# Layer 1's second operand group in other homes and another order, one raw weight load later, and one token pair's transposes one product later

## The chip, the cores and the metric

The kernel runs on one core of a Trainium2 chip. The core has five engines that run their own instruction streams side by side: TensorE (PE, matmuls and transposes, with a separate line for its weight loads, PEld), VectorE (DVE), ScalarE (ACT), GpSimd (POOL) and SyncE (SP, which here issues the DMAs). They wait for one another by semaphores. The metric is the time of one execution on the device in microseconds (us), lower is better.

## The reference, cut to what is computed

One layer of an encoder: two groups of heads side by side (a bidirectional mLSTM and a latent attention), a projection of their outputs, and a feed-forward part. Sequence 2048, model width 1024, hidden width 4096, all in float32.

```python
h = rms_norm(x, g_mix_norm[l])
z = h @ w_in[l]
q_m, k_m, v_m, o_m, gates, c_q, c_kv, k_pe = jnp.split(z, splits, axis=-1)
...
y_a = mlstm_group(q_m, k_m, v_m, o_m, gates, b_gates[l], g_mlstm_out[l])
y_b = mla_group(c_q, c_kv, k_pe, cos, sin, g_cq[l], g_ckv[l], w_uq[l], w_ukv[l],
                g_q[l], g_k[l])
x = x + jnp.concatenate([y_a, y_b], axis=-1) @ w_out[l]
h = rms_norm(x, g_ffn_norm[l])
x = x + jnp.square(jax.nn.relu(h @ w_ff1[l])) @ w_ff2[l]
```

The change lies in the last three lines: in the projection by `w_out`, and in the product by `w_ff1`, which the kernel calls layer 1. Layer 2 is the product by `w_ff2`.

## The kernel before

**Arithmetic.** A float32 operand is split into a high part, rounded to the matmul's type, and a low part, the rest. ACT writes the high part (a copy, L53 or L1455, L1819, L1881), DVE the low part (a subtraction, L54 or L47). A product is the sum of three matmuls, high by high, high by low and low by high (`mm3`, L68 to L71). The three large products (projection, layer 1, layer 2) are block products in the manner of Strassen and Winograd: seven products of half-size blocks in place of eight, where some operands are sums and differences of blocks, named S1 to S4 and T1 to T4, beside the plain blocks A11, B21 and so on.

**Order.** From the projection on, the program order is written by hand: each engine executes its instructions in the order in which the Python code issues them, and waits only where data or memory requires it. Python code that stands later on the page can thus hold an engine up only if it is later on the same engine.

**Projection (class OutProj, `run`).** Sixteen token tiles of 128 rows go in eight pairs, `PAIRS`; the first is done plainly, and the loop over n = 1 to 7 does seven products for each other pair. Between the products the loop issues the work of the neighbours: for pair n the operands (`cast`, `low`, `combine`), for pair n - 1 (named p, with the token tiles a1 and b1) the sum with x (`add`, L1407), the store, the norm (`squares`, POOL's root, `scale`, L1495) and the transposition of the normalised rows: `transpose_n` (L1505, four PE transposes of half a token tile into the one PSUM buffer `dpt`) and `evacuate_n` (L1509, DVE, out of that buffer and times the gain). Pair p's normalised blocks then go through `combine_store` to DRAM (`d_h`), as the seven operands of layer 1. With n = 2, p is the first pair that takes this way, and product 6 of pair 1 stands between products 1 and 2 of pair 2. In the last round, n = 7 (`LAST`), the loop also reads back and splits layer 1's operands (`h_load` L1853, `h_split`) and loads the first two raw weight blocks (`load_w1`, L1795, two loads of 512 KB for a unit).

**Layer 1 (class FeedForward, `layer1`).** The tokens are done in two groups of 1024, and the hidden width in 16 units of 256, so there are 32 units n, each of seven products p; the first group has units 0 to 15, the second 16 to 31. Product p reads operand p of the token group (`self.H[p]`) and the weights of the unit (`weights1`, a generator that splits them some products ahead and forms S1 to S4 by `w1_combine`, L1809). `evacuate` takes each product out of PSUM (DVE L1943, ACT L1946 and L1947), `u_combine` (L1980) forms layer 2's operands and `u_store` (L1974) sends them to DRAM (`d_u`).

The seven operands of a group lie in seven **homes**, pairs of high and low tiles named after `HSLOT`: B11, B21, T2, T1, T3, B22, B12, in this order for operands 0 to 6 of the first group. T1, T2 and T3 are in one pool (`f_h0`), the B homes in another (`f_h1`) on the other side of memory. The second group is brought in by the generator `exchange`, which runs over units 14 to 16: operand 0 goes to stage buffers, operand 1 to the ring, and operands 2 to 6 into the homes that the first group's products 0 to 4 of unit 15 leave one by one (B11, B21, T2, T1, T3). Each is loaded into the home's low tile (L1885, two loads), and `place`, called once per product, casts one half to the high tile (L1881) and subtracts it from the half before (L47). The list `todo` sets the order of these splits.

**Layer 2 (`layer2`).** It has 112 units of 24 matmuls (8 blocks of three). Its first two units are prepared early: `first2` loads them in unit 31, and `opening()`, called after product 4 of unit 31, closes the pool of T1, T2, T3 and opens the pools of layer 2 (`open2`) in the memory so freed, with the splits of the first two units into `uh`, `ul`, `w2h`, `w2l`. In program order, these splits stand ahead of the evacuations of products 4, 5 and 6 of unit 31. `start2` then closes the pool of the B homes and issues the loads of the third unit (L2091, L2097, L2144), and `layer2` issues those of unit n + 3 in unit n.

Of the kernel before, what the change touches and what calls it, by code (L numbers as in the profile page):

```python
# [1288 lines left out]
class OutProj:  # L1289
# [229 lines left out]
    def run(self, ff):  # L1519

        nc = self.c.nc
        LAST = len(self.PAIRS) - 1
        self.sw, self.xp = ff.sw, ff.r1p
        pieces = [(op, k) for op in range(7) for k in range(4)]

        def h_load(n):
            for _ in range(n):
                i = 28 - len(pieces)
                ff.h_load(0, *pieces.pop(0), self.c.e[:, i - 4, :] if 4 <= i < 8 else None)

        def h_split(n):
            for _ in range(n):
                ff.h_split()

        self.prep_y(1)
        for s in (2, 3):
            self.load_y(s)
        self.load_b2(1)
        for s in range(2):
            self.load_x(s)  # L1540
        self.load_b2(0)
        for s in (2, 3):
            self.load_x(s)
        tops = self.t_operands(ff.hp)

        def t_op(n):
            for _ in range(n):
                next(tops, None)

        self.project(0, [(j, k) for k in range(KD) for j in range(2)])  # L1550
        t_op(4)
        for s in (2, 3):
            self.transpose_y(s)
        self.project(1, [(j, k) for j in (1, 0) for k in range(KD)])
        t_op(2)
        self.cast(1, "A11")
        self.combine(1, "S1")
        self.low()
        self.combine(1, "S3")
        t_op(1)  # L1560
        self.cast(1, "A12")
        self.cast(1, "S1")
        self.low()
        self.low()
        t_op(1)
        for j in range(2):
            self.add(0, j, ("plain", 0, j), True)
        self.store(0)

        comb = iter(())  # L1570
        for n in range(1, LAST + 1):
            m, p = n + 1, n - 1
            a, b = 2 * n, 2 * n + 1
            a1, b1 = a - 2, b - 2
            a2, b2 = a + 2, b + 2
            norm, norm1, more = 1 <= n <= 4, 1 <= p <= 4, n < LAST

            self.product(n, 0)
            if n > 1:
                self.add(b1, 1, (p, "A"))  # L1580
            else:
                for j in (1, 0):
                    self.add(1, j, ("plain", 1, j), True)
                self.store(1)
            if norm1:
                self.scale(a1)
            self.combine(n, "S2")
            if n == 1:
                t_op(1)
            next(comb, None)  # L1590

            if n == LAST - 1:
                ff.load_w1(0)
            if n == 2:
                self.product(n, 1)
            elif n > 2:
                self.product(p, 6)
            if norm1:
                self.transpose_n(0)
            self.add(a, 0, (n, "A"))  # L1600
            if n == 2:
                t_op(2)
                self.product(p, 6)
            self.cast(n, "S2")
            self.cast(n, "A22")
            self.low()
            self.combine(n, "S4")
            self.low()
            self.cast(n, "S4")
            next(comb, None)  # L1610
            if more:
                self.load_y(a2)
                self.load_y(b2)
            else:
                ff.load_w1(1)
                h_load(2)

            if n != 2:
                self.product(n, 1)
            if norm1:  # L1620
                self.evacuate_n(a1, 0)
                self.transpose_n(1)
            if n > 1:
                self.add(b1, 0, (p, "A"), True)
                self.store(b1)
            if norm1:
                self.squares(b1)
            self.low()
            for _ in range(2):
                next(comb, None)  # L1630
            if n == 1:
                t_op(1)
            if n == LAST:
                h_split(2)

            self.product(n, 2)
            self.add(a, 0, (n, "B"), True)
            self.cast(n, "S3")
            if norm1:
                self.scale(b1)  # L1640
                self.evacuate_n(a1, 1)
                self.transpose_n(0)
            if n == 1:
                t_op(2)
            if n == LAST:
                h_split(3)
            if n >= LAST - 1:
                h_load(2 if more else 4)

            self.product(n, 3)  # L1650
            self.add(*((b, 1, (n, "C")) if more else (a, 1, (n, "A"))))
            self.low()
            if norm1:
                self.evacuate_n(b1, 0)
                self.transpose_n(1)
            if more:
                self.transpose_y(a2)
                self.transpose_y(b2)
                self.load_x(a2)
            if n == 1:  # L1660
                t_op(1)
            if n == LAST:
                h_split(3)
            if n >= LAST - 1:
                h_load(2)

            self.product(n, 4)
            self.add(*((a, 1, (n, "A")) if more else (b, 1, (n, "C"))))
            if more:
                self.cast(m, "A11")  # L1670
                self.combine(m, "S1")
                self.low()
                self.combine(m, "S3")
                self.load_x(b2)
            if norm1:
                self.evacuate_n(b1, 1)
            if n == 1:
                t_op(1)
            if n == LAST:
                ff.wsteps = ff.weights1()  # L1680
                next(ff.wsteps)
                h_split(3)
            if n >= LAST - 1:
                h_load(2 if more else 3)

            self.product(n, 5)
            if more:
                self.add(a, 1, (n, "C"), True)
                self.store(a)
            else:  # L1690
                self.add(b, 1, (n, "A"))
            if more:
                self.cast(m, "A12")
                self.cast(m, "S1")
                self.low()
                self.low()
            if norm:
                self.squares(a)
            if norm1:
                comb = self.combine_store(p)  # L1700
            next(comb, None)
            if n == 1:
                t_op(1)
            if n == LAST:
                for _ in range(3):
                    next(ff.wsteps)
                h_split(3)
            if n >= LAST - 1:
                h_load(2 if more else 3)

        self.product(LAST, 6)
        self.add(a, 1, (LAST, "C"))
        self.store(a)
        for _ in range(2):
            next(ff.wsteps)
        h_split(2)
        h_load(2)
        next(ff.wsteps)
        self.add(b, 0, (LAST, "A"))
        self.store(b)  # L1720
        next(ff.wsteps)
        return pieces
# [41 lines left out]
class FeedForward:  # L1764
# [58 lines left out]
    def weights1(self):  # L1823

        N = 2 * self.NU
# [4 lines left out]
        for s in range(7 * N + 1):  # L1830
            if last:
                last()
                self.nsplit += 1
            last = self.w1_split(*divmod(s, 7)) if s < 7 * N else None
            yield
            n, q = divmod(s - 1, 7)
            if s and q == 0:
                self.w1_combine(n, "S3")
            elif s and q == 2:
                self.w1_combine(n, "S4")  # L1840
            elif q == 4 and n + 1 < N:
                self.w1_combine(n + 1, "S1")
            elif q == 5 and n + 1 < N:
                self.w1_combine(n + 1, "S2")
            elif s and q == 6 and n + 2 < N:
                self.load_w1(n + 2)
            yield

# [19 lines left out]
    def exchange(self):  # L1868
# [3 lines left out]
        todo = []  # L1872
# [24 lines left out]
        for _ in range(4):  # L1897
            place()
            yield
        nxt = [first, [[t[:, k, :] for t in s for k in range(2)] for s in second]]  # L1900
        for p in range(13):
            if p < 5:
                hi, lo = self.h_slot(p)
                nxt.append([[t[:, k, :] for k in range(4)] for t in (hi, lo)])
                for k in range(0, 4, 2):
                    load(hi[:, k:k + 2, :], lo[:, k:k + 2, :], c.d_h[1, p + 2, :, k:k + 2, :])
            if p < 7:
                self.H[p] = nxt[p]
            place()
            yield  # L1910
# [364 lines left out]
```

## Time and profile before

| | us |
|---|---|
| median of 3 runs | 2565.96 |
| lowest to highest | 2564.87 to 2566.89 |
| profiled execution, whole time | 2567.94 |
| its span | 2566.1 |
| mean granted clock of TensorE in it | 0.998 |

The profile comes from one execution. Its page gives the busy time of each engine and, for groups of instructions of one line, the mean duration and the idle time of the engine just before them with what ended it. The stages in time, by PE's rows of its timeline: the projection runs from about 1155 to 1327, layer 1 from 1327.32 to 1944.83, layer 2 from there to the end. Row by row, the timeline shows start, duration, engine, line, operation, the names of what is written and read, and in brackets the idle time ahead and its releaser.

### The profile page before, as it was taken

Reading aid. Unit: us, or ns where it says so; the run is one execution under the profiler, and the core shown is the slowest. Engines: PE = TensorE matmul, PEld = TensorE weight load, DVE = VectorE, ACT = ScalarE, POOL = GpSimd, SP = SyncE. Lnnn points to the kernel's source line nnn. Section 1 sums busy time; section 2 is a strip of 40 time slices with the busy share of each in tenths; the row PEclk is TensorE's granted clock in tenths of the full one; section 3 lists DMA queues with packets and bytes.
Section 4 is the critical chain, followed back from the end, with each engine's and each line's share of the span. In section 5 each row is a group of like instructions: output and inputs, shape, how many; then the busy total and the mean of one; then the engine's idle time right before and its main releaser. Section 6 shows DMA issues by size and latency. Waiting matters only on the chain. (4 is left out here: it accounts for less than half of the span.)

```text
span 2566.1 us, 37087 instructions
## 1 busy us (share of the span) xinstructions
PE 2541.2 (99%) x13148; PEld 2155.2 (84%) x13148; DVE 1726.2 (67%) x3300; ACT 1248.3 (49%) x2517; POOL 385.4 (15%) x430
## 2 busy tenths in 40 slices
PE   9999999999999999999999999999999999999999
PEld 7888888888888888898888888888887888888887
DVE  4585467766676667678788777977774577666443
ACT  5554444546656656565445555655553323332332
POOL 1111111123224214110100000000000233222000
PEclk9999999999999999999999999999999999999999
DMA  5434234356446454535786655744447644444552
GB/s 172 144 111 151 91 117 135 95 135 128 102 87 134 94 111 105 89 103 191 218 283 208 200 198 177 251 162 151 144 152 270 214 148 142 148 143 146 213 180 95
DMA packets 301790, 393.67 MB, mean 153 GB/s; under 512 B 33125, under 2 KB 186788, under 8 KB 301604
## 3 DMA queue, kind: packets, MB, share of 16 engines
q1 hardware_dynamic: 299140, 386.84, 50.1%
q10 hardware_dynamic: 2464, 4.46, 0.5%
q8 instruction: 103, 1.69, 0.3%
q14 instruction: 83, 0.68, 0.1%
HBM read 259.04 MB, written 132.17 MB: 152 GB/s over the span
## 5 line engine op out<-in xcount | busy, mean ns | idle before, releaser
L69 PE MATMUL pd<-w2h,uh 128*128 128x512 f32 x896 | 349.4, 390 | 3.5 <-DVE e L1943 3.5
L70 PE MATMUL pd<-w2l,uh 128*128 128x512 f32 x896 | 349.2, 390 | 1.8 <-DVE w2l L54 1.8
L71 PE MATMUL pd<-w2h,ul 128*128 128x512 f32 x896 | 349.0, 390 | 0.0
L54 DVE TENSOR_TENSOR ul<-ur,uh 128x1024 fp32r<-128x1024 f32 x110 | 146.9, 1335 | 254.7 <-ACT uh L53 254.6
L53 ACT CAST uh<-ur 128x1024 fp32r<-128x1024 f32 x110 | 116.0, 1055 | 397.2 <-PE pd L70 385.0
L54 DVE TENSOR_TENSOR ptl<-ptp,pth 128x512 fp32r<-128x512 f32 x252 | 173.6, 689 | 174.5 <-ACT pth L53 165.6
L53 ACT CAST pth<-ptp 128x512 fp32r<-128x512 f32 x252 | 146.4, 583 | 240.5 <-PE ptp L1120 235.2
L1943 DVE TENSOR_TENSOR e<-pu,e 128x512 f32<-128x512 f32 x224 | 150.9, 687 | 89.1 <-PE pu L71 88.1
L1080 DVE TENSOR_SCALAR_CACHE_REDUCE p<-ps 128x512 f32<-128x512 f32 x256 | 174.8, 683 | 47.1 <-PE ps L1079 39.0
L69 PEld LDWEIGHTS pd<-w2h,uh 128*128 128x128 f32 x896 | 168.6, 188 | 38.9 <-DVE e L1943 3.9
L70 PEld LDWEIGHTS pd<-w2l,uh 128*128 128x128 f32 x896 | 168.6, 188 | 37.2 <-DVE w2l L54 2.2
L71 PEld LDWEIGHTS pd<-w2h,ul 128*128 128x128 f32 x896 | 168.5, 188 | 35.1
L2107 POOL TENSOR_TENSOR r<-wr,r 128x512 f32<-128x512 f32 x48 | 86.3, 1797 | 622.0 <-DVE w2l L54 452.3
L69 PE MATMUL pz<-wh,hh 128*128 128x512 f32 (+1 forms) x384 | 150.1, 392 | 2.1 <-ACT hh L53 0.7
L1120 PE MATMUL ptp<-ident,p 128*128 128x128 f32 x1008 | 151.3, 273 | 0.7 <-ACT p L1091 0.7
L71 PE MATMUL pz<-wh,hl 128*128 128x512 f32 (+1 forms) x384 | 150.4, 392 | 0.0
L70 PE MATMUL pz<-wl,hh 128*128 128x512 f32 (+1 forms) x384 | 149.9, 391 | 0.1
L70 PE MATMUL pv<-ptl,vh 128*128 128x256 f32 x496 | 140.4, 283 | 1.4 <-DVE ptl L54 1.3
L1946 ACT ACTIVATE e<-e 128x512 f32<-128x512 f32 x128 | 80.9, 632 | 122.8 <-DVE e L1943 116.2
L71 PE MATMUL pv<-pth,vl 128*128 128x256 f32 x496 | 140.0, 282 | 0.0
L69 PE MATMUL pv<-pth,vh 128*128 128x256 f32 x496 | 139.9, 282 | 0.0
L1091 ACT ACTIVATE p<-p,nm 128x2048 f32<-128x2048 f32 x64 | 128.5, 2008 | 19.7 <-DVE nm L1084 19.7
(526 smaller groups left out, 6591.6 us busy)
## 6 DMA issues: line engine op xcount, KB each, us to landing
d_u<-e SPq DMA_DIRECT2D x224, 256.0 KB
ur<-d_u SPq DMA_DIRECT2D x110, 512.0 KB
wr<-in_w SPq DMA_DIRECT2D x96, 256.0 KB
w1raw<-in_w SPq DMA_DIRECT2D x42, 512.0 KB
raw<-in_w_in SPq DMA_DIRECT2D x48, 256.0 KB
r<-in_w SPq DMA_DIRECT2D x22, 512.0 KB
mb<-d_M SPq DMA_DIRECT2D x32, 256.0 KB
acc<-d_x SPq DMA_DIRECT2D x16, 512.0 KB
```

What stands on the lines that cost most here:

```text
L53: r = nc.scalar.copy(hi, src)
L54: (eng or nc.vector).tensor_tensor(lo, src, hi.bitcast(F32), op=ALU.subtract)
L69: nc.tensor.matmul(out, ah, bh, start=first, stop=False, skip_group_check=more)
L70: nc.tensor.matmul(out, ah, bl, start=False, stop=False, skip_group_check=more)
L71: nc.tensor.matmul(out, al, bh, start=False, stop=last, skip_group_check=more)
L1080: nc.vector.tensor_scalar(probs[b, a][:, j, :], o, SCALE, None, op0=ALU.mult, op1=ALU.max, accum_out=maxes[b, a][:, j:j + 1])
L1091: nc.scalar.activation(p, p, AF.Exp, bias=maxes.pop((b, a)), accum_out=dens[b][:, a:a + 1])
L1120: nc.tensor.transpose(pt[:, k, :], p[:, j, k * P:(k + 1) * P], c.ident)
L1943: nc.vector.tensor_tensor(out, o, t, op=ALU.add)
L1946: nc.scalar.activation(t, t, AF.Relu)
L2107: nc.gpsimd.tensor_tensor(R, wr, R, op=ALU.subtract)
```

## The change

It has three parts. None adds or removes an instruction; all move instructions within program order, and the second group's operands get other homes.

In the projection, only with n = 2: the four transposes of each half token tile, their evacuations and `scale(b1)` are issued one product later than before. The first transposes come after product 6 of pair 1, the last after product 4 of pair 2, and the last evacuation after product 5.

```diff
-            if norm1:
+            if norm1 and n > 2:
                 self.transpose_n(0)
             self.add(a, 0, (n, "A"))
             if n == 2:
                 t_op(2)
                 self.product(p, 6)
+                self.transpose_n(0)
...
-            if norm1:
+            if norm1 and n > 2:
                 self.evacuate_n(a1, 0)
                 self.transpose_n(1)
...
             self.cast(n, "S3")
-            if norm1:
+            if n == 2:
+                self.evacuate_n(a1, 0)
+                self.transpose_n(1)
+                self.scale(b1)
+            elif norm1:
                 self.scale(b1)
                 self.evacuate_n(a1, 1)
                 self.transpose_n(0)
...
-            if norm1:
+            if n == 2:
+                self.evacuate_n(a1, 1)
+                self.transpose_n(0)
+            elif norm1:
                 self.evacuate_n(b1, 0)
                 self.transpose_n(1)
...
-            if norm1:
+            if n == 2:
+                self.evacuate_n(b1, 0)
+                self.transpose_n(1)
+            elif norm1:
                 self.evacuate_n(b1, 1)
...
+            if n == 2:
+                self.evacuate_n(b1, 1)
```

The raw weights of layer 1's unit 1 are loaded after product 6 of the last pair and not after its product 0, and the two combinations of that unit that come first, S1 and S2, are formed one step later each.

```diff
             else:
-                ff.load_w1(1)
                 h_load(2)
...
         h_split(2)
         h_load(2)
+        ff.load_w1(1)
         next(ff.wsteps)
...
-            elif q == 4 and n + 1 < N:
+            elif q == 4 and n and n + 1 < N:
                 self.w1_combine(n + 1, "S1")
             elif q == 5 and n + 1 < N:
-                self.w1_combine(n + 1, "S2")
+                self.w1_combine(n + 1, "S2" if n else "S1")
             elif s and q == 6 and n + 2 < N:
+                if n == 0:
+                    self.w1_combine(1, "S2")
                 self.load_w1(n + 2)
```

In `exchange`, the homes B11, B21, T2, T1, T3 are filled, at the same moments as before, with operands 5, 6, 2, 3, 4 and not with 2, 3, 4, 5, 6. The splits come in the order 5, 2, 3, 4, 6.

```diff
-        nxt = [first, [[t[:, k, :] for t in s for k in range(2)] for s in second]]
+        nxt = {0: first, 1: [[t[:, k, :] for t in s for k in range(2)] for s in second]}
+        late = []
         for p in range(13):
             if p < 5:
+                op = (5, 6, 2, 3, 4)[p]
                 hi, lo = self.h_slot(p)
-                nxt.append([[t[:, k, :] for k in range(4)] for t in (hi, lo)])
+                nxt[op] = [[t[:, k, :] for k in range(4)] for t in (hi, lo)]
                 for k in range(0, 4, 2):
-                    load(hi[:, k:k + 2, :], lo[:, k:k + 2, :], c.d_h[1, p + 2, :, k:k + 2, :])
+                    load(hi[:, k:k + 2, :], lo[:, k:k + 2, :], c.d_h[1, op, :, k:k + 2, :])
+                if op == 6:
+                    late = [todo.pop() for _ in range(2)][::-1]
+                elif op == 4:
+                    todo += late
```

## The prediction

> **What bounds the kernel now.** First the busy times of the page, then the list of waits of TensorE (PE), longest first, of which these six lie in the stages that the change touches.
>
> ```profile
> PE 2541.2 (99%) x13148; PEld 2155.2 (84%) x13148; DVE 1726.2 (67%) x3300; ACT 1248.3 (49%) x2517; POOL 385.4 (15%) x430
> ...
> PE pd L69 <- DVE e L1943: 3.5, 1, 3.5
> PE pd L70 <- DVE w2l L54: 1.8, 1, 1.8
> PE dpt L1505 <- DVE e L1509: 1.0, 1, 1.0
> PE po L69 <- DVE e L1407: 0.9, 1, 0.9
> PE dpt L1505 <- ACT e L1495: 0.8, 1, 0.8
> PE pu L70 <- DVE T3l L47: 0.6, 1, 0.6
> ```
>
> PE is the bound: 99% busy, so the change adds and removes no matmul and can only move these 8.6 us of waiting, and what each wait drags along. The largest two stand where layer 1 ends and layer 2 begins, so I read that place first, on PE.
>
> ```profile
> 1944.83 0.39 PE L69 MATMUL pd<-w2h,uh 128*128 128x512 f32 x1
> 1947.04 0.50 PE L70 MATMUL pd<-w2l,uh 128*128 128x512 f32 x1 [1.82 <-DVE w2l L54]
> 1947.38 0.39 PE L71 MATMUL pd<-w2h,ul 128*128 128x512 f32 x1
> 1951.24 0.80 PE L69 MATMUL pd<-w2h,uh 128*128 128x512 f32 x1 [3.47 <-DVE e L1943]
> ...
> 1957.64 0.39 PE L69 MATMUL pd<-w2h,uh 128*128 128x512 f32 x1
> 1968.52 0.39 PE L69 MATMUL pd<-w2h,uh 128*128 128x512 f32 x1
> 1951.00:1955.00 4.00, 3.76 (x10) 3.01 (x11) 2.02 (x4) 2.03 (x4) 0.00 (x0) 0.56 0.87 275
> ```
>
> A unit of layer 2 has 24 matmuls. Units 1 and 2 fill 1957.64 to 1968.52, so a matmul takes 10.88 / 48 = 0.227 us from start to start (the 0.39 is its length in the pipeline; an idle of x therefore costs x + 0.16). Unit 0 would need 24 x 0.227 = 5.44 us and took 1957.64 - 1944.83 = 12.81: **7.37 us are lost here**, more than the 5.3 us of idle, because after the long wait the granted clock (last row, third figure from the end) is 0.56 until 1955.
>
> Why it waits is on the DVE and ACT rows, with one PE row that dates the product before the last two of layer 1 (operand 4, in home T2).
>
> ```profile
> 1945.09 1.29 DVE L54 TENSOR_TENSOR ul<-raw,uh 128x512 fp32r<-128x512 f32 x2 [6.93 <-issue]
> ...
> 1948.71 2.48 DVE L1943 TENSOR_TENSOR e<-pu,e 128x512 f32<-128x512 f32 x4
> 1939.36 1.14 ACT L53 CAST uh<-raw 128x512 fp32r<-128x512 f32 x2 [3.19 <-PE pu L70]
> 1945.03 1.14 ACT L53 CAST uh<-raw 128x512 fp32r<-128x512 f32 x2 [4.00 <-PE pu L71]
> 1936.67 0.39 PE L69 MATMUL pu<-T2h,r 128*128 128x512 f32 x1
> ```
>
> ACT casts uh for unit 0 when the last read of T2 ends (1936.67 + 2.49 + 0.39 = 1939.5 for the product, L70 a little sooner), and uh for unit 1 only when the very last product of layer 1, on T3, ends at 1945.0. DVE stands idle 6.93 us before its first low part, because ul, too, lies in T3's memory. Behind the six low parts wait four L1943, the evacuations of the last three products of layer 1; the last ends at 1951.19, and PE's second block of layer 2 starts right then.
>
> **The change, part by part.** All sums are against the profiled execution (span 2566.1, whole time 2567.94, 1.98 above the median 2565.96).
>
> *Homes of the second group.* Operands 2, 3, 4 now lie in T2, T1, T3 and 5, 6 in B11, B21. No instruction is added: the same ten loads and ten casts in another order. The three T homes are last read by the products of operands 2, 3 and 4, so all are free at 1939.5, when before T1 and T3 were busy up to 1942.3 and 1945.0. Then: ACT's six casts (two of 1.14 for a pair, 0.6 for a weight) end by 1941.1 to 1942.6; DVE's six low parts, one per 0.60 us by the row (1945.09 to 1948.71 is 3.62 us), run from 1939.5 to 1943.1, beside the last two products. L1943 starts at 1943.1 instead of 1948.71: two for operand 4, one for 5 at about 1944.4, and the one for 6 as soon as its product ends, 1945.05 to 1945.75. PE: the first L70 no longer waits; the second block waits at most to 1945.8 (it would be due at 1945.5), and with so short a wait I take the clock as full. Unit 0 ends at 1945.8 + 21 x 0.227 = 1950.56: **-7.1 us** (ends: 0 if the wait had another cause, -7.37 if none is left).
>
> What is late next is the data of units 2 and 3, whose loads follow those evacuations on SP.
>
> ```profile
> 1951.15 0.38 SPq L2091 DMA_DIRECT2D ur<-d_u  x1
> ...
> 1957.84 0.74 SPq L2091 DMA_DIRECT2D ur<-d_u  x1
> 1965.83 0.68 DVE L54 TENSOR_TENSOR w2l<-r,w2h 128x512 fp32r<-128x512 f32 x1
> ```
>
> The first load stands behind the store of operand 4's result, the second behind five more stores; all move with L1943, by 5.6 us. Unit 3's last low part then ends at 1966.51 - 5.6 = 1960.9, and PE wants it at 1968.52 - 7.1 + 0.23 = 1961.65. The margin falls from 2.2 to 0.7 us: covered, and if that cover goes, one for one.
>
> *Order of the exchange's splits.* Operand 6 is still cast last, so the wait at T3l goes over to B21l. DVE is what it waits for:
>
> ```profile
> 1656.65 1.22 DVE L47 TENSOR_TENSOR T3l<-T3l,T3h 128x1024 fp32r<-128x1024 f32 x1
> ```
>
> It stands in DVE's queue in the same place after the same work, so **0** (from -0.8, gone, to +1, if operand 4, which takes operand 5's old slots, comes late).
>
> *Unit 1's raw load (L1795), past product 6 of the last pair.* PE's 0.9 us there comes from L1407, which stands in DVE's queue behind T2's low parts, and these behind late loads.
>
> ```profile
> 1311.56 1.03 SPq L1795 DMA_DIRECT2D w1raw<-in_w  x2
> 1322.42 0.62 ACT L53 CAST T2h<-raw 128x512 fp32r<-128x512 f32 x1 [1.30 <-DMA raw<-d_h]
> 1323.08 0.69 DVE L54 TENSOR_TENSOR T2l<-raw,T2h 128x512 fp32r<-128x512 f32 x1 [1.19 <-ACT T2h L53]
> 1323.69 0.68 DVE L1407 TENSOR_TENSOR e<-po,e 128x512 f32<-128x512 f32 x1
> 1320.00:1324.00 4.00, 3.55 (x16) 2.62 (x14) 2.67 (x5) 2.70 (x6) 0.00 (x0) 1.00 1.05 397
> 1337.51 1.22 ACT L53 CAST B12h<-raw 128x512 fp32r<-128x512 f32 x2 [1.37 <-DMA raw<-d_h]
> 1340.05 1.29 DVE L54 TENSOR_TENSOR B12l<-raw,B12h 128x512 fp32r<-128x512 f32 x2
> ```
>
> Two loads of 512 KB ahead of T2's, with the DMA engines full at 397 GB/s, are 1.05 MB / 397 = 2.6 us; without them T2 lands that much sooner, L1407 loses its 1.19 us, and PE gains 0.9 + 0.16 = 1.06. The 2.6 us come back later: the loads now go out near 1330, ahead of operand 6's (B12), which ACT already waits for at 1337.51. DVE takes B12's low parts only at 1340.05, 2.5 us after the cast, so most is hidden; I charge 0.2. The combinations S1 and S2 of unit 1 move one step, same instructions, used only by unit 1. **-0.9** (from -1.06 to +1.5, if all 2.6 reach PE).
>
> *The pair's transposes one product later.* Removed are the waits of 1.0 and 0.8, with 0.16 each: -2.1. What comes in their place:
>
> ```profile
> 1200.29 0.60 PE L1505 MATMUL dpt<-ident,e 128*128 128x128 f32 x4
> 1206.28 0.68 DVE L1509 TENSOR_TENSOR e<-dpt,vec 128x512 f32<-128x512 f32 x1
> 1216.11 0.68 DVE L1509 TENSOR_TENSOR e<-dpt,vec 128x512 f32<-128x512 f32 x1
> 1216.13 0.39 PE L69 MATMUL po<-T3h,r 128*128 128x512 f32 x1
> ```
>
> Product 6 starts at 1200.29, then come four transposes (some 0.45) and product 2, so the next transposes are due at 1206.2; the L1509 before them, one slot of 0.60 earlier than at 1206.28 since another L1509 ahead of it is gone, ends at 1206.36: 0.2 lost. Then a **new wait**: the second half of the second token tile is transposed after product 4, and its L1509 stands where the last L1509 stood, behind the next pair's S1 and S3. That one ended at 1216.79, when product 5 had begun at 1216.13: 0.7 lost. What is queued behind on PE is product 5. Sum -2.1 + 0.2 + 0.7 = **-1.2** (from -2.1 to 0).
>
> Sum: -7.1 - 0 - 0.9 - 1.2 = -9.2 us, 2567.94 - 9.2 = 2558.7 in a profiled run, **2556.8** against the median.
>
> **A rule weighed against the rows.** These two windows lie in the attention stage.
>
> ```profile
> 473.00:476.00 3.00, 1.01 (x8) 0.61 (x8) 1.87 (x8) 2.75 (x6) 0.00 (x0) 1.00 0.61 161
> 478.00:480.00 2.00, 2.00 (x8) 1.71 (x7) 1.97 (x7) 0.84 (x2) 0.00 (x0) 0.51 0.07 1
> ```
>
> About 2 us of idle within 3 us brought the clock to 0.51 soon after. So the clock can fall without one long wait; in my forecast no 3 us hold more than 1 us of idle. If it falls once all the same, it costs what it costs at the boundary, 1957.64 - 1951.24 - 21 x 0.227 = 1.6 us: 2558.4, inside my range. The Trainium skill, "TensorE: Matmul & The Clock Gate", section "What's actually happening", has the rate halved after an idle window of about 3.4 us and back after as long a busy one. By that rule the new waits could cost nothing more than themselves, and the sum stays; the window at 473 disagrees with it (2 us sufficed), so the measurement decides.
>
> **The rivals.**
> 1. *Late data takes the wait's place.* Units 2 and 3 of layer 2 come later than 5.6 us sooner, or B12 reaches PE. For: a margin of 0.7 us, DMA engines at 0.87 and more. Against: the loads' own chain moves by 5.6 of PE's 7.1 us, and 0.7 is left. 1 to 4 us back: 2558 to 2561, middle 2559.8.
> 2. *The boundary stays as it is* (the change doesn't do what it says): ul and the second uh lie in memory that operands 5 and 6 now hold. Against: ACT's two releasers are exactly T2's and T3's last reads. 2565.96 - 2.1 = 2563.9.
> 3. *Slower:* unit 1's load, now behind others, holds ACT, in order, at its first cast, with B12's casts queued behind it, and product 6 of unit 0 stands. Each us of landing past the turn of that cast is a us of PE; it decides from 8.3 us on. At 13 us late, with one loss of clock, 13 + 1.6 - 8.3 = +6.3: 2572.3. Against: at 397 GB/s that is 5 MB more than is in flight.
>
> **How the numbers follow.** Forecast 0.71 (own range 2554.8 to 2558.6), rival 1 0.14, rival 2 0.11, rival 3 0.04. A measurement of this kernel can tell about 0.2%, 5.1 us, from no change, so faster means below 2560.8: 0.71 + 0.11 of rival 1 = 0.82; same 0.03 + 0.11 = 0.14; slower 0.04. The range, 2554.6 to 2561.2, leaves out 0.18.
>
> **What would show it.** Right: the waits pd L70 <- w2l and po L69 <- L1407 gone, pd L69 <- L1943 below 0.5, granted clock 1.00 throughout the boundary, L54 on DVE from about 1939 in the old count, a wait of 0.6 at B21l, one new dpt L1505 <- L1509 of about 0.7 before product 5. Wrong: a pd wait for L54 of units 2 or 3, a pu wait for B12 in unit 0, or the old 3.5 us still there.

## The result and the profile after

| | before | after |
|---|---|---|
| median of 5 runs each, side by side on one chip, us | 2564.87 | 2555.24 |
| lowest to highest | 2563.51 to 2566.89 | 2554.31 to 2559.31 |
| profiled execution, whole time | 2567.94 | 2554.74 |
| its span | 2566.1 | 2553.0 |

The ratio is 0.9964, with a 95% interval of 0.995 to 0.9979: faster by 0.21 to 0.5%. The forecast was 2556.8 and faster.

The two profiled spans differ by 13.1 us, which is more than the change made. PE's first matmul of the projection shows it. The columns of the timeline are start, duration, engine, line, operation, names written and read, and in brackets the idle time ahead with its releaser. First before:

```profile
1154.84 0.48 PE L69 MATMUL po<-B11h,r 128*128 128x512 f32 x1
```

Then after, with the first matmul of layer 1 below it (1327.32 before):

```profile
1150.71 0.48 PE L69 MATMUL po<-B11h,r 128*128 128x512 f32 x1
1320.91 0.39 PE L69 MATMUL pu<-B11h,r 128*128 128x512 f32 x1
```

4.13 us of the difference lie ahead of the projection, where the program is the same: one execution simply differs from another there (the last section shows where most of it arises). So from here on I compare **stages**, each from the first matmul of it on PE to the first of the next:

| stage, us | before | after | |
|---|---|---|---|
| projection | 172.48 | 170.20 | -2.27 |
| unit 0 of layer 1 | 19.04 | 19.06 | +0.02 |
| units 1 to 14 | 273.84 | 274.01 | +0.18 |
| units 15 and 16 | 39.01 | 39.00 | -0.01 |
| units 17 to 31 | 285.62 | 285.60 | -0.02 |
| first unit of layer 2 (the boundary) | 12.81 | 5.88 | -6.93 |
| the rest of layer 2 | 608.48 | 608.49 | 0.00 |

The sum is -9.05 with unrounded lengths; the forecast's sum was -9.2. After's list of waits of PE, of which these two lie in the changed stages, below its page's row of busy times:

```profile
PE 2535.8 (99%) x13148; PEld 2151.7 (84%) x13148; DVE 1725.6 (68%) x3300; ACT 1247.5 (49%) x2517; POOL 378.7 (15%) x430
...
PE dpt L1505 <- DVE e L1509: 0.6, 1, 0.6
PE pu L70 <- DVE B21l L47: 0.6, 1, 0.6
```

The instruction counts are those of before. The two pd waits and the po wait are gone; T3l has become B21l; of the dpt waits one is left, and it is a new one.

**The boundary after**, on PE, on ACT, DVE and SP, and as a window (its third figure from the end is the granted clock). After's line numbers are up to 21 higher: L1964 is L1943 of before, L2112 is L2091. Layer 2 begins at 1938.59, so a time of after stands 6.24 us below its counterpart of before.

```profile
1938.59 0.39 PE L69 MATMUL pd<-w2h,uh 128*128 128x512 f32 x1
1938.81 0.39 PE L70 MATMUL pd<-w2l,uh 128*128 128x512 f32 x1
1939.04 0.39 PE L71 MATMUL pd<-w2h,ul 128*128 128x512 f32 x1
1939.55 0.50 PE L69 MATMUL pd<-w2h,uh 128*128 128x512 f32 x1
...
1944.47 0.39 PE L69 MATMUL pd<-w2h,uh 128*128 128x512 f32 x1
...
1933.35 1.14 ACT L53 CAST uh<-raw 128x512 fp32r<-128x512 f32 x2 [1.87 <-PE pu L71]
...
1933.40 1.29 DVE L54 TENSOR_TENSOR ul<-raw,uh 128x512 fp32r<-128x512 f32 x2 [1.49 <-issue]
...
1937.02 2.48 DVE L1964 TENSOR_TENSOR e<-pu,e 128x512 f32<-128x512 f32 x4
...
1939.47 0.38 SPq L2112 DMA_DIRECT2D ur<-d_u  x1
...
1954.25 0.68 DVE L54 TENSOR_TENSOR w2l<-r,w2h 128x512 fp32r<-128x512 f32 x1
...
1955.57 0.39 PE L70 MATMUL pd<-w2l,uh 128*128 128x512 f32 x1
...
1938.00:1942.00 4.00, 3.88 (x18) 2.86 (x17) 2.05 (x4) 3.32 (x6) 0.00 (x0) 1.00 0.55 162
```

The reader is to see that the low parts now start some 5 us before layer 2 does (1933.40) and not with it, that the four evacuations end at 1939.50, and that the second block of layer 2 follows right then, at 1939.55. It would have been due at 1938.59 + 3 x 0.227 = 1939.27, so it starts 0.28 late, where before the two waits held PE idle for 5.3 us, and the clock stays at 1.00. The low part for layer 2's unit 3 ends at 1954.93, where PE reads it at 1955.57: a margin of 0.64.

### The profile page after: what moved, and what is told of

It reads as the page before. It is cut to its first block, busy times and chain, and to the rows that moved or that the text cites. A ratio compares the mean times of both kernels' runs of the same rounds, so it can differ in the third digit from the quotient of the medians.

```text
span 2553.0 us, 37087 instructions
## 1 busy us (share of the span) xinstructions
PE 2535.8 (99%) x13148; PEld 2151.7 (84%) x13148; DVE 1725.6 (68%) x3300; ACT 1247.5 (49%) x2517; POOL 378.7 (15%) x430
## 5 line engine op out<-in xcount | busy, mean ns | idle before, releaser
L69 PE MATMUL pd<-w2h,uh 128*128 128x512 f32 x896 | 348.7, 389 | 0.1
L1964 DVE TENSOR_TENSOR e<-pu,e 128x512 f32<-128x512 f32 x224 | 150.8, 686 | 88.9 <-PE pu L71 87.9
L69 PEld LDWEIGHTS pd<-w2h,uh 128*128 128x128 f32 x896 | 168.2, 188 | 35.4 <-DVE e L1964 0.5
L2128 POOL TENSOR_TENSOR r<-wr,r 128x512 f32<-128x512 f32 x48 | 80.9, 1686 | 621.6 <-DVE w2l L54 445.4
L69 PE MATMUL pz<-wh,hh 128*128 128x512 f32 (+1 forms) x384 | 149.4, 390 | 1.7 <-ACT vo L495 0.7
L69 PE MATMUL pv<-pth,vh 128*128 128x256 f32 x496 | 140.0, 282 | 0.1
```

The costliest lines, as they stand in the source:

```text
L69: nc.tensor.matmul(out, ah, bh, start=first, stop=False, skip_group_check=more)
L1964: nc.vector.tensor_tensor(out, o, t, op=ALU.add)
L2128: nc.gpsimd.tensor_tensor(R, wr, R, op=ALU.subtract)
```

## The experiments

The kernels ran in groups, each group on one chip together with the kernel before. The median of the kernel before was 2567.6 to 2570.3 there, according to the chip (2564.87 in the table above), so whole times are set against the kernel before on the same chip, and the argument goes by stages. My theory is the prediction's; its rivals stand in each expectation.

### The three parts one by one

**The homes alone.** The kernel before with the third part of the change:

```diff
+                op = (5, 6, 2, 3, 4)[p]
...
-                    load(hi[:, k:k + 2, :], lo[:, k:k + 2, :], c.d_h[1, p + 2, :, k:k + 2, :])
+                    load(hi[:, k:k + 2, :], lo[:, k:k + 2, :], c.d_h[1, op, :, k:k + 2, :])
```

> The kernel before with the new homes and the new order of splits alone. Theory (the homes free T3, and with it the first low parts of layer 2): the stretch from layer 2's first matmul to that of its unit 1, 12.81 us before and 5.88 after, becomes 5.9; projection stays at 172.5 us, unit 16 at 20.0. Rival (the boundary owes part of its gain to the earlier arrival or to less DMA traffic from the other two parts): it stays above 7.

Measured: boundary 5.86 (-6.95), unit 0 19.04, 2562.47 against 2569.78. The homes carry the boundary by themselves. One thing was not foreseen: the projection took 171.88 instead of 172.48, though nothing of it was changed, because the wait po L69 <- L1407 was 0.3 in this execution and not 0.9. What the load's move can win is itself not constant.

**The load alone.**

```diff
-                ff.load_w1(1)
                 h_load(2)
...
         h_load(2)
+        ff.load_w1(1)
```

> The kernel before with unit 1's raw load later alone. Theory (the 1 MB ahead of T2's loads held L1407 up): PE's wait of 0.9 us before the last pair's product 6 goes, the projection stage falls from 172.48 by 1.0 to 1.1 us, unit 0 of layer 1 keeps its 19.04 us within 0.1, the boundary stays at 12.8. Rival (T2's loads are late for the stores ahead of them): the wait stays, or goes over to another operand, and the stage falls by less than 0.4.

Measured: 2569.09 against 2569.78, one execution each; projection 171.29 (-1.19), but unit 0 19.70 (**+0.66**) and units 1 to 14 +0.13. This kernel's rows on DVE and PE (layer 1 starts at 1326.69; L1809 forms a combination, L1945 is the evacuation):

```profile
1338.41 0.69 DVE L1809 TENSOR_TENSOR sw<-w1raw,w1raw 128x512 f32<-128x512 f32 x1 [1.50 <-DMA w1raw<-in_w]
...
1345.65 0.69 DVE L1945 TENSOR_TENSOR e<-pu,e 128x512 f32<-128x512 f32 x1
...
1346.39 0.50 PE L69 MATMUL pu<-B11h,w1raw 128*128 128x512 f32 x1 [0.39 <-DVE e L1945]
```

DVE stands in front of unit 1's S1 until the raw load has landed, everything behind it in its queue comes late, and so does an evacuation for whose PSUM buffer PE waits at unit 1's first matmul. In after the same wait is there, 1.71 us long, and costs PE nearly nothing:

```profile
1332.01 0.69 DVE L1822 TENSOR_TENSOR sw<-w1raw,w1raw 128x512 f32<-128x512 f32 x1 [1.71 <-DMA w1raw<-in_w]
```

The gain ahead of layer 1 is smaller in its cause than forecast. After's casts of T2 on ACT:

```profile
1311.82 1.29 ACT L53 CAST T2h<-raw 128x512 fp32r<-128x512 f32 x2 [0.49 <-DMA raw<-d_h]
...
1315.17 0.62 ACT L53 CAST T2h<-raw 128x512 fp32r<-128x512 f32 x1 [2.07 <-DMA raw<-d_h]
```

The third stands 164.46 us behind the projection's first matmul, and 167.58 in before (1322.42 - 1154.84): 3.12 us sooner, of which the shorter transposes make 1.07. About 2.0 are left for the load's move (1.84 in load alone, by the same count), not 2.6, which was still enough for L1407 and PE.

What DVE's wait costs in layer 1 depends on how late S1 starts, counted from layer 1's first matmul: 11.10 us here (1332.01 - 1320.91), 11.72 there.

**The transposes alone.**

```diff
                 self.product(p, 6)
+                self.transpose_n(0)
```

> The kernel before with the pair's later transposes alone. Theory (two waits of 0.97 and 0.76 go, one of 0.64 comes and one of 0.2): the projection stage falls from 172.48 by 1.1 to 1.3 us, the boundary stays at 12.8. Rival (the new wait of 0.64 belongs to the three parts together): the stage falls by 2 us.

Measured: 2569.24 against 2569.78, one execution each; projection 171.29 (-1.19). The wait po L69 was 0.7 here instead of 0.9, so about -1.07 belongs to the transposes. The new wait is where it was forecast; the rows are after's:

```profile
1202.29 0.66 PE L1505 MATMUL dpt<-ident,e 128*128 128x128 f32 x4
...
1209.59 0.68 DVE L1509 TENSOR_TENSOR e<-dpt,vec 128x512 f32<-128x512 f32 x1
...
1210.42 0.63 PE L1505 MATMUL dpt<-ident,e 128*128 128x128 f32 x4 [0.64 <-DVE e L1509]
```

The two boundaries that kept their homes show a further thing: 13.84 (load alone) and 13.32 (transposes alone) for the same waits of 1.8 and 3.5 that stand in the 12.81 of before. The waits are equal; what differs is when the clock fell (last section).

### What the boundary waits for

**T3 again the last home that is filled.** After, with this order:

```diff
-                op = (5, 6, 2, 3, 4)[p]
+                op = (5, 2, 3, 4, 6)[p]
```

> The kernel after, but T3 holds operand 6 as before the change, with 5, 2, 3, 4 in B11, B21, T2, T1. Theory (only T3's last read holds the first low parts back): the boundary goes back from 5.88 to about 12.8 us, with the waits of about 1.8 and 3.5 us and the clock near 0.56 behind them. Rival (B21 and T1, or the order of the splits, make the gain): it stays below 8.

Measured: boundary 13.21, with both waits back (PE's timeline of this kernel):

```profile
1943.14 0.50 PE L70 MATMUL pd<-w2l,uh 128*128 128x512 f32 x1 [1.82 <-DVE w2l L54]
...
1947.34 0.80 PE L69 MATMUL pd<-w2h,uh 128*128 128x512 f32 x1 [3.47 <-DVE e L1959]
```

It is the operand in T3, and its last reader, that the boundary waits for.

**T1 holds operand 5, T3 stays free early.**

```diff
-                op = (5, 6, 2, 3, 4)[p]
+                op = (3, 6, 2, 5, 4)[p]
...
-                if op == 6:
-                    late = [todo.pop() for _ in range(2)][::-1]
+                if op > 4:
+                    late = [todo.pop() for _ in range(2)][::-1] + late
```

> The kernel after, but T1 holds operand 5, as before the change, and B11 operand 3; T3 still holds 4. Theory (only T3 counts, T1's memory goes to buffers that are loaded later): the boundary stays at 5.9 us. Rival (each T home holds something back): it rises by 2.7 us, a product's length, or more.

Measured: boundary 5.90, so T1 doesn't count there. But units 15 and 16 took 43.16 instead of 39.00, **+4.14**: with operand 3 in B11 and 5 split later, operand 4's cast moved ahead in ACT's queue, to a place where its load had not landed. This kernel's ACT and PE, and its windows:

```profile
1642.68 1.05 ACT L1896 CAST T3h<-T3l 128x1024 fp32r<-128x1024 f32 x1 [3.05 <-DMA T3l<-d_h]
...
1659.26 0.76 PE L70 MATMUL pu<-B21l,r 128*128 128x512 f32 x1 [1.99 <-DVE B21l L47]
...
1654.00:1658.00 4.00, 2.74 (x11) 1.61 (x9) 3.96 (x7) 2.52 (x4) 0.00 (x0) 1.00 0.59 177
1658.00:1662.00 4.00, 2.74 (x7) 2.17 (x8) 4.00 (x7) 1.77 (x3) 0.00 (x0) 0.67 0.84 288
1662.00:1666.00 4.00, 4.00 (x18) 3.28 (x17) 3.84 (x8) 3.10 (x6) 0.00 (x0) 0.91 0.62 229
```

A wait of 3.05 us on ACT that ends at 1642.68 reaches PE up to 17 us later, as waits of 0.67, 0.53 and 1.99, the last two on another operand, B21l, at the end of DVE's queue: DVE, kept from its low parts for 3.7 us, was busy 3.96 and 4.00 of 4 us in the first two windows and had no room to catch up. The idle of 0.53 and 1.99 within 4.2 us then cost the clock as well: 0.67 and 0.91, and units 17 to 31 took 0.56 more. It is the end "operand 4 comes late" of the forecast's second step, and it costs four times the bound given there.

### What is left in the projection and in units 15 and 16

**The evacuation first.** After, with n = 2's evacuation and transposes issued ahead of the next pair's operands:

```diff
+            if n == 2:
+                self.evacuate_n(b1, 0)
+                self.transpose_n(1)
             if more:
                 self.cast(m, "A11")
                 self.combine(m, "S1")
...
-            if n == 2:
-                self.evacuate_n(b1, 0)
-                self.transpose_n(1)
```

> The kernel after, with the evacuation and the transposes that stand after product 4 of pair 2 issued ahead of the next pair's first casts and not behind them. Theory (PE's new wait of 0.64 us is only DVE's queue): the wait goes, the projection stage falls from 170.20 by 0.8 us. Rival (DVE is short of time there, and the next pair's operands come late instead): it falls by less than 0.3, with a wait at a later product.

Measured: projection 169.38 (-0.82 against after), and no dpt wait is left in this kernel's list. The wait came from the queue ahead of L1509. Unit 0 took 19.43: the load again.

**One low part on GpSimd.** After, where operand 6's first low part (B21l) goes to POOL; in DVE's queue it stands ahead of the second one, for which PE waits 0.6:

```diff
-            place()
+            place(nc.gpsimd if p == 11 else None)
```

> The kernel after, with the low part of operand 6's first half (unit 16) subtracted on GpSimd and not on DVE. Theory (PE's wait of 0.6 us at B21l is DVE's backlog): unit 16 falls from 19.96 us by 0.8 to 19.2. Rival (the wait hangs on ACT's cast of the second half or on a load): it stays at 19.9; or GpSimd, at some 3.6 us for this size, is itself late, and the wait moves to the first half and grows.

Measured: units 15 and 16 39.48 (+0.48), the wait 1.1 instead of 0.6. This kernel's POOL and DVE:

```profile
1648.52 2.98 POOL L1894 TENSOR_TENSOR B21l<-B21l,B21h 128x1024 fp32r<-128x1024 f32 x1 [87.68 <-ACT B21h L1897]
...
1648.02 1.22 DVE L1894 TENSOR_TENSOR T3l<-T3l,T3h 128x1024 fp32r<-128x1024 f32 x1
1649.15 0.68 DVE L1965 TENSOR_TENSOR e<-pu,e 128x512 f32<-128x512 f32 x1
1649.75 2.30 DVE L1822 TENSOR_TENSOR sw<-sw,w1raw 128x512 f32<-128x512 f32 x1
```

DVE was to gain 1.2 us and lost 0.5: its L1822 took 2.30 instead of the usual 0.68 beside POOL. The second low part of B21 started 0.48 later in unit 16 than in after, and PE's wait grew by 0.48. It follows DVE's queue one for one, though not in the direction that I had meant.

**The sums later.** The same wait from the other side: two sums of unit 15's result move behind the low part.

```diff
-    SUMS = ..., {4: ["S1", "S2"], 5: ["S4"], 6: ["S3"]}
+    SUMS = ..., {5: ["S4"], 6: ["S3"]}
...
+                    if p == 5:
+                        self.u_combine(n - 1, "S1")
+                        self.u_combine(n - 1, "S2")
```

> The changed kernel with the two sums S1 and S2 of unit 15's result, which stand in DVE's queue in unit 16 ahead of the low part for which PE waits 0.6 us, moved behind that low part. Theory (that wait is a matter of DVE's queue alone): the low part comes some 1.4 us sooner, the wait of PE at operand 1's low part is gone, unit 16 of layer 1 lasts 19.2 instead of 19.96 us, nothing else changes: -0.8 us. Rival (the wait only moves): the evacuations that stand behind come later by the same 1.4 us and PE waits for one of them, so that units 15 and 16 together stay within 0.3 us of 39.0.

Measured: units 15 and 16 38.08 (**-0.92** against after), no wait at B21l. After's rows of DVE and PE show what was ahead of that low part:

```profile
1648.53 1.40 DVE L2001 TENSOR_TENSOR e<-e 128x512 f32<-128x512 f32 x2
1649.85 0.68 DVE L47 TENSOR_TENSOR r<-w1raw,r 128x512 fp32r<-128x512 f32 x1
1650.45 1.22 DVE L47 TENSOR_TENSOR B21l<-B21l,B21h 128x1024 fp32r<-128x1024 f32 x1
...
1651.72 0.50 PE L70 MATMUL pu<-B21l,r 128*128 128x512 f32 x1 [0.63 <-DVE B21l L47]
```

So the wait takes neither other homes nor another order of the splits to remove: it is enough to take these 1.40 us of sums (L2001) out of DVE's queue ahead of the low part. Unit 0 took 19.64, again by the load.

### The load and its cover

S1 of unit 1 on DVE, in the kernels that hold the load where the change put it, and what unit 0 lost over 19.04:

| kernel | S1 starts after layer 1's first matmul, us | unit 0 loses |
|---|---|---|
| one low part on GpSimd | 10.98 | 0.00 |
| T1 holds operand 5 | 10.99 | 0.00 |
| after | 11.10 | 0.02 |
| the evacuation first | 11.46 | 0.39 |
| T3 holds operand 6 | 11.60 | 0.53 |
| the sums later | 11.67 | 0.60 |
| the load alone | 11.72 | 0.66 |

The loss is the start less 11.07, within 0.02 wherever there is one. Nothing in these programs differs between the projection's end and S1; the landing of the load does, by 0.7 us. SP issues it 2.70 to 3.61 us into layer 1, but the issue alone doesn't set the order: after's is the earliest, and its S1 is only third.

**S1 one step later**, together with S2:

```diff
-            elif q == 5 and n + 1 < N:
-                self.w1_combine(n + 1, "S2" if n else "S1")
+            elif q == 5 and n and n + 1 < N:
+                self.w1_combine(n + 1, "S2")
             elif s and q == 6 and n + 2 < N:
                 if n == 0:
+                    self.w1_combine(1, "S1")
                     self.w1_combine(1, "S2")
```

> The changed kernel with S1 of layer 1's unit 1 formed one step later still, together with S2. Theory (the later raw load stands at the edge of its cover: DVE waits 1.5 to 2.2 us for it at S1, and behind S1 stands the evacuation for which PE waits at the first product of unit 1 whenever S1 starts later than 11.07 us after layer 1's first matmul): DVE's wait of 1.5 to 2.2 us in front of S1 is gone or below 0.5, PE has no wait at that product, unit 0 of layer 1 lasts 19.04 us within 0.05. Rival (DVE and ACT merely wait for the same queue of transfers one step later, at operand 6's low parts): unit 0 again above 19.3 or units 1 to 14 above 274.2, with a PE wait for operand 6 or for S1 itself, which then comes too late for the products that read it. Whole time: the changed kernel's 2555 to 2560 either way; the stage decides.

The theory's numbers missed: unit 0 took 20.40, **+1.36**. ACT and PE of this kernel:

```profile
1342.13 1.28 ACT L53 CAST B12h<-raw 128x512 fp32r<-128x512 f32 x2 [3.14 <-DMA raw<-d_h]
...
1343.84 0.58 ACT L1972 COPY e<-pu 128x512 f32<-128x512 f32 x1
1344.47 0.50 PE L69 MATMUL pu<-B12h,r 128*128 128x512 f32 x1 [0.58 <-ACT e L1972]
...
1347.80 0.50 PE L69 MATMUL pu<-B11h,w1raw 128*128 128x512 f32 x1 [0.31 <-DVE e L1965]
```

Here S1 started only at 12.85, after 1.66 us of waiting in its later place, and operand 6's cast stood 14.72 us into the layer (12.97 in after). Behind that cast, on ACT, an evacuation for PE was queued: close to the forecast's slower rival, and small. But what ACT stood for here was operand 6's own load; for unit 1's weights it had waited 1.18 us before. The weights and operand 6 came some 1.8 us later than in after, and a later S1 is no cure for that.

**Three moves together:** the evacuation first, the sums later, and S1 later.

> The changed kernel with three moves together: the evacuation and the transposes of the projection's second pair ahead of operand A11's work, S1 of layer 1's unit 1 one step later, and unit 15's two sums behind operand 1's low part. By the theories: projection -0.8 (169.4 us), unit 0 19.04, unit 16 19.2 instead of 19.96, boundary 5.88 as it is: 1.6 us less than the changed kernel, some 2553.5 us, ratio to the kernel before 0.9955 with an interval that overlaps that of the changed kernel. If the waits only move: projection 170.2, unit 16 19.96, whole time as the changed kernel's 2555.2.

Measured: 2560.18 against 2570.33 on its chip, ratio 0.9958 (0.9945 to 0.9972). Projection 169.39, unit 0 19.04, units 15 and 16 38.08. S1 started at 11.49 and unit 0 lost nothing, where the table above would have had 0.42 (the evacuation first lost 0.39 at 11.46): in this one execution a later S1 bought that much.

**The load one product sooner,** behind product 5 of the last pair, where T2's blocks have landed:

```diff
                 h_split(3)
             if n >= LAST - 1:
                 h_load(2 if more else 3)
+            if n == LAST:
+                ff.load_w1(1)
...
-        ff.load_w1(1)
         next(ff.wsteps)
```

> The changed kernel with the raw loads of unit 1 issued one product sooner than in the changed kernel: after the last pair's product 5, behind the loads issued there, and not after its product 6. Theory (T2's loads are what must not stand behind them, and these have landed 4 us before; the loads then jump about 1 MB of other transfers, 2.6 us at 400 GB/s, and S1 finds them landed): T2's first cast stays 8 to 9 us ahead of layer 1's first matmul, projection 170.2 us as in the changed kernel, DVE's wait in front of S1 gone or below 0.5 us, S1 at most 10.5 us after layer 1's first matmul, unit 0 of layer 1 at 19.04. Rival (the transfers that are jumped are wanted just as soon): a PE wait for operand 5 or 6 (B22 or B12) in unit 0, or for the last sums of the projection, so that projection and unit 0 together are not below 189.3 us.

Measured: projection 170.23, unit 0 19.04, units 1 to 14 273.84 as in before. On DVE S1 no longer waits, and ACT waits elsewhere, for operand 5's second half, at no cost to PE:

```profile
1333.96 0.68 DVE L1823 TENSOR_TENSOR sw<-w1raw,w1raw 128x512 f32<-128x512 f32 x1
...
1335.26 1.26 ACT L53 CAST B22h<-raw 128x512 fp32r<-128x512 f32 x2 [4.39 <-DMA raw<-d_h]
```

S1 starts at 1333.96 - 1324.66 = 9.30 us, 1.8 ahead of the edge.

**The best of them:** the evacuation first, the sums later, the load one product sooner.

> The changed kernel with three moves: the second pair's evacuation and transposes ahead of operand A11's work, the raw loads of unit 1 one product sooner, and unit 15's two sums behind operand 1's low part. By the stages: projection 169.4 us (-0.8), unit 0 19.04, units 15 and 16 38.08 (-0.9), boundary 5.86: 1.7 us less than the changed kernel's profiled execution and up to 3.1 less than the executions of the changed program in which unit 0 lost 0.4 to 1.3; ratio to the kernel before 0.9955 within 0.0015. Against: a wait for operand 5 or 6 in unit 0 of 0.5 us or more.

Measured: 2556.70 against 2567.57 on its chip, ratio 0.9956 (0.9943 to 0.997). By stages: projection 169.37, unit 0 19.05, units 1 to 14 273.84, units 15 and 16 38.08, boundary 5.86; no wait of po, dpt, pu or pd is left in PE's list. Its stages are 1.96 us shorter than after's; the intervals of the two ratios overlap, so the whole times alone don't tell them apart.

## Why the prediction was right, point by point

1. **Homes, -7.1: measured -6.93, alone -6.95.** Each time of its chain, less the 6.24, was met: low parts from 1933.26 (measured 1933.40), evacuations from 1936.86 (1937.02), the last one's end at 1939.51 (1939.50), unit 3's margin 0.7 (0.64). The missing 0.15 is in PE's rows: for the first matmuls after the short wait the pitch is 0.23 to 0.34 and not 0.227.
2. **Order, 0: measured -0.01**, wait 0.63, moved from T3l to B21l. The reason given, DVE's queue, holds: two sums taken out of it removed the wait (-0.92), a longer operation in it lengthened it. The bound of +1 for a late operand 4 was too small; it came to 4.14.
3. **Raw load, -0.9: measured -1.0** (projection -2.27 + 1.07, then +0.02 + 0.18). The size came out, but the step "the combinations S1 and S2 of unit 1 move one step, same instructions" was incomplete. The forecast looked for the returning delay at B12; it came at S1 itself, where DVE's wait holds up the evacuation that PE needs. The 0.2 that I charged hit the profiled execution by luck: in those of the other kernels with the load and S1 in these places it was 0.05 to 0.8. I had not named what hides S1's wait: in its new place S1 starts at 9.30 when it needn't wait (the load one product sooner), so its cover is 11.07 - 9.30 = 1.8 us. T2's loads came some 2.0 us sooner and not 2.6.
4. **Transposes, -1.2: measured -1.07.** The new wait before product 5 was 0.64 and cost 0.80 with its 0.16 (0.7 lost in the forecast) and the small one 0.19 (0.2 forecast, PE's matmul at 1202.29).
5. **The sum, -9.2: -9.05 in one profiled execution,** and -9.63 between the medians measured side by side. The measured time lies 1.6 below the forecast; 1.1 of it is that the kernel before, run beside after, had a median of 2564.87 and not the 2565.96 from which I had counted.
6. **The clock.** The forecast had no clock loss, and the window above shows 1.00. The disagreement of the row at 473 with an idle window of 3.4 us is seen once more: no idle stretch above 1.99 us, and the clock fell, where operand 5 lay in T1. In before, too, it fell at the boundary at 1947.70, when only the first wait of 1.82 was over: the long wait, after which the prediction puts the low clock, began at 1947.77. What the runs add is the spread: the same two waits of 1.8 and 3.5 us made a boundary of 12.81, 13.21, 13.32 or 13.84, so the 7.1 of the first step belonged to one execution. The Trainium skill, "TensorE: Matmul & The Clock Gate", section "What's actually happening", has the window run freely, not started by the kernel, so that the moment at which the clock changes, counted from the first matmuls, varies by 0.5 us either way. The trace agrees that it runs freely; the moment differs by up to 2.11 us at the boundary here, as the last section works out.
7. **Rivals.** Late data in layer 2 did not come: 0.64 us of margin held. "The boundary stays" is what T3 holding operand 6 does, so its mechanism was the right one to fear. Of the slower one, a late load that holds ACT with operand 6 behind it, there is a relative in S1 one step later: ACT waited for the weights and then for operand 6 itself, and an evacuation behind that made PE wait 0.58, which costs about 0.7 us and not 6.

## What to carry to other kernels

Where one engine is 99% busy, a change is worth the waits that it removes, each with the clock loss behind it, which is not the same in every execution. Here the sum from the timeline came within 0.2 us of the profiled execution. Every cover has to be named for that: the one place where I named none is the one that varied. A load that is moved later has to be judged by the first instruction in order that waits for it and by what is queued behind that, on each engine; if its margin is below a microsecond, one profile can't tell whether it holds. Compare stages of two profiles, not their spans: the unchanged part differed by 4.13 us here.

## What the runs showed that was not expected

**GpSimd beside DVE.** In the rows of that experiment, POOL ran from 1648.52 to 1651.50. DVE's L1965, which reads one operand from PSUM, took its usual 0.68 in that time, but L1822, with both operands in SBUF, ended only at 1652.05, 0.55 after POOL did by a row whose span is rough. The Trainium skill, "SBUF — State Buffer", section "SBUF: two separate sides", says that a DVE operation with two SBUF inputs and a GpSimd operation that reads SBUF lock each other out for the whole instruction; the rows agree. If POOL itself stood until DVE's 1.22 us subtraction ended at 1649.24, 2.26 of its 2.98 us were work, which is an estimate; DVE takes 1.22 for the same.

**The unchanged part is not constant.** From the start to the projection's first matmul the 14 profiled executions took 1150.71 to 1157.16 us, on several chips, with the same program there. That is two thirds of what the change brings. Of the 4.13 us between before and after, 1.98 have gathered by 13 us into the execution: after's 128x464 matmuls take 0.37 us from 8.31 on, before's from 12.41 on, and about 0.6 ahead of that. Another 1.57 come between 476 and 480.5, where the granted clock falls to 0.50 in before and stays at 1.00 in after.

**When the clock falls.** Two windows of before around the boundary's first wait and, last, one of the evacuation first, in the attention stage. Behind the length stands PE's busy time, and third from the end the granted clock:

```profile
1944.29:1947.70 3.41, 1.59 (x7) 0.72 (x5) 2.61 (x5) 1.66 (x3) 0.00 (x0) 1.00 0.00 0
1947.70:1954.52 6.82, 3.35 (x9) 2.62 (x9) 4.84 (x9) 3.58 (x6) 0.00 (x0) 0.50 0.44 136
...
471.69:475.10 3.41, 1.73 (x10) 1.30 (x11) 2.50 (x8) 2.33 (x6) 0.00 (x0) 1.00 0.48 128
```

In all 14 profiled executions the changes of the granted clock lie whole multiples of 3.413 us apart; in before, the falls at 476.55 and 1947.70 are 431 of them apart. So I divide the traces into stretches of that length, up to the end of PE's work. The clock fell after each of the 14 stretches at full clock in which PE's rows leave 1.82 us or more idle (first row: 3.41 - 1.59), and after none of the other 10397, which leave 1.68 (last row) or less. About half a stretch sufficed, with the idle time in pieces. Where the boundary kept its two waits, the clock then stood at 0.50 for two stretches, and what differs is how much of this lies behind the second wait, which ends 6.41 us into layer 2 in all four:

| kernel | clock falls, us into layer 2 | at 0.50 behind the waits | boundary | boundary less half of that |
|---|---|---|---|---|
| before | 2.87 | 3.28 | 12.81 | 11.17 |
| T3 holds operand 6 | 3.63 | 4.05 | 13.21 | 11.18 |
| transposes alone | 3.92 | 4.33 | 13.32 | 11.15 |
| the load alone | 4.98 | 5.40 | 13.84 | 11.14 |

The last column is the same within 0.04 us, so the spread of the boundary is the place of the stretches and nothing else that shows. By these four executions the homes are worth 6.9 to 8.0 us.

**A load's landing is not constant either.** Issued 2.7 to 3.6 us into layer 1, unit 1's weights let S1 start 10.98 to 12.85 us into it, with the DMA engines full: in after the window below (DMA share 1.06, 379 GB/s) holds all of DVE's wait for them.

```profile
1328.00:1332.00 4.00, 4.00 (x19) 3.32 (x18) 2.29 (x4) 1.73 (x3) 0.00 (x0) 1.00 1.06 379
```

What makes one execution's transfers slower than another's stays open; no run was made for it.
